# The first layer's feed-forward by Strassen's 2x2 form, with its context rows in two plain passes and one PSUM tile for each product

## The chip, the cores and the metric

The kernel runs on one core of a Trainium2 chip. The metric is the device time of one execution in microseconds (us), as the median of several runs. TensorE (called PE in the profile, with PEld for its weight loads) multiplies a 128x128 weight tile by up to 512 columns at a time into PSUM. VectorE (DVE), ScalarE (ACT) and GpSimd (POOL) do the elementwise work, and SyncE (SP) issues all the transfers of this kernel, in the order of the program.

## The reference, cut to what matters

A trunk of two layers runs over 1024 latent tokens and 256 context tokens, with 1024 features each. Each layer has a mixer and then a gated feed-forward with 2816 hidden features:

```
def swiglu(h, w_in, w_out):
    g, u = jnp.split(h @ w_in, 2, axis=-1)
    return (jax.nn.silu(g) * u) @ w_out

for i in range(DEPTH):                      # DEPTH = 2
    ...                                     # mixer, gated residual
    hl = modulate(rmsnorm(xl, norm_ffn_g[i]), sh2_l, sc2_l)
    xl = xl + g2_l * swiglu(hl, ffn_w_in[i], ffn_w_out[i])
    if not last:
        xc = xc + g1_c * yc
        hc = modulate(rmsnorm(xc, norm_ffn_g[i]), sh2_c, sc2_c)
        xc = xc + g2_c * swiglu(hc, ffn_w_in[i], ffn_w_out[i])
return rmsnorm(xl, norm_final_g)
```

The context goes through the feed-forward in the first layer only, since nothing reads it after the second layer's mixer. All data are fp32. The products must be nearly as exact as fp32, so every operand is split into a high and a low part in the format that TensorE multiplies fast.

## The kernel before, in words

Everything is kept with features on the partitions: `x[d]` is one 128-feature tile of the residual, `h[k]` one of the normed input. Tokens come in three chunks: chunk 0 is the context (256 columns), chunks 1 and 2 are the two halves of the latents (512 columns each). `Row.v(c)` is a tile's part for chunk c.

A weight unit is a 128x1024 tile, eight 128x128 blocks. The class `Stream` (`ws`, lines 205 to 256) hands units out in the one order that is written into `ws.src`: it loads a unit with a transfer into a `raw` buffer (two of these), splits it with `split` (line 258) into `whi` (a copy on ACT, line 259) and `wlo` (a difference on DVE, line 260), and keeps three units split ahead. Every product of a block is three matmuls (lines 329, 330 and 331): high by high, high by low, low by high. So a unit costs 24 matmuls for each chunk that it meets.

The first layer's feed-forward is `ffn` (lines 784 to 830). For each f of the 22 tiles of hidden features it multiplies the gate unit and then the up unit with all three chunks, and after every two f it multiplies the two output units with the hidden tiles and adds each product to `x[d]` on DVE (line 824). Two hidden tiles (f) are thus 6 units, each of which meets three chunks, and 432 matmuls; all 22 are 4752 matmuls, of which 3168 have 512 columns and 1584 have 256.

The second layer's feed-forward works on the latents only and uses Strassen's form with 7 products in place of 8 (lines 1161 to 1364). Weight units are quartered (classes `Block` and `Rows`), quarters are added and subtracted on DVE as they are needed (lines 159 to 165 and 193 to 202), and the input halves are combined once (`h_sums`). For each f there are 7 products of 4 blocks, 84 matmuls of 512 columns (loop at 1262); their results are combined by ACT copies (lines 1273, 1278, 1280, 1282 and 1288) and DVE additions (1275, 1283, 1285, 1286 and 1289). The accumulators are `a`, a PSUM tile of its own, and `b` and `c`, the two halves of one two-bank tile `pb`. Hidden tiles go to DRAM by pairs, again in 7 combinations (`pair_jobs`, `thid`), and the output projection reads them back (`Right`, line 1242) for 77 quarter units of 12 matmuls, 924 matmuls in all (loop at 1327). The first two f of this layer are done plainly, to cover the norm before them.

Small work is interleaved from two lists: `bg` and `slow`. `step(n, m)` runs up to n jobs of the first (a `None` ends the call) and m of the second. `slow` holds the modulation parameters of the next layer (`ada_slow`, lines 408 to 451): 96 loads of 256 KB, 96 groups of DVE multiply-adds (lines 431 and 433), and 24 finishing jobs, each of which transposes on TensorE what DVE has summed (line 438) and reduces it on DVE (439). A norm is a job of statistics on TensorE, ACT and DVE (`Norm.stat`), a broadcast on TensorE (line 498) and eight `norm_apply` jobs (lines 512, 505 and 506). `Norm.feed` squares on ACT and sums on POOL (line 470). Except for SP, whose order is the program's, the order on an engine comes from a planner that goes by the order of the program and by when it believes operands and buffers to be ready.

## Time and profile before

| | us |
|---|---|
| median of 3 runs | 2648.4 |
| the three runs | 2647.07, 2648.4, 2654.0 |
| the profiled execution's own time | 2644.94 |
| its span, first to last instruction | 2643.2 |
| first layer's feed-forward, first to last matmul | 526.37 to 1456.36 |
| second layer's feed-forward, 20 Strassen blocks | about 2018 to 2409 |
| its output projection by Strassen | about 2409 to 2626 |

The span is what the trace covers; the execution's own time is 1.7 us more. Matmuls overlap: each takes about 0.39 us from start to end, but they start much closer together, so the cost of one is the distance between two starts. A busy TensorE in the profile says only that no gap longer than the overlap was seen.

### The profile page before, as it was taken

The numbers are of one execution on the slowest core, as the hardware profiler recorded it, in microseconds if no ns is written. First come the engines' busy times: TensorE is split into PE (matmuls) and PEld (weight loads), VectorE is DVE, ScalarE is ACT, GpSimd is POOL, SyncE is SP. The second block draws the span as 40 slices with busy tenths as digits, with TensorE's granted clock in tenths as the row PEclk, the third lists the DMA queues.
The fourth block names the chain that finished last, engine by engine and source line by source line (L and its number), as shares of the span: only waits on it lengthen the run. The fifth ranks groups of instructions, "written<-read, shape, count | busy, mean of one in ns | idle before, by whom it ended". The sixth has DMA issues, their size and how long they took to land.

```text
span 2643.2 us, 33892 instructions
## 1 busy us (share of the span) xinstructions
PE 2523.7 (95%) x12730; PEld 2103.6 (80%) x12730; DVE 1740.3 (66%) x3182; ACT 1063.3 (40%) x1852; POOL 369.2 (14%) x344
## 2 busy tenths in 40 slices
PE   6999999999999999999999979989999999999997
PEld 3777888788888888888887867778887777777876
DVE  7779857565554554445447658998869556657765
ACT  6685422341111111111115437787745333334453
POOL 2231102200000000000002216555610000000001
PEclk9999999999999999999999999999999999999998
DMA  6112315222122211221112274533252332338352
GB/s 233 56 61 92 104 56 205 74 96 72 44 84 80 80 58 55 88 84 65 67 48 96 97 182 117 128 84 113 91 180 88 104 108 88 105 108 299 98 169 79
DMA packets 134212, 273.39 MB, mean 103 GB/s; under 512 B 13216, under 2 KB 39968, under 8 KB 134048
## 3 DMA queue, kind: packets, MB, share of 16 engines
q1 hardware_dynamic: 134048, 271.22, 31.1%
q8 instruction: 100, 1.64, 0.3%
q14 instruction: 64, 0.52, 0.1%
HBM read 225.82 MB, written 45.35 MB: 103 GB/s over the span
## 4 chain that ended last, share of the span: by engine, by line
PE 77%; DVE 13%; ACT 4%; issue 3%; DMA 3%; POOL 1%; SPq 0%; DVEq 0%; ACTq 0%; POOLq 0%
PE pa L330 14%; PE pa L329 14%; PE pa L331 13%; PE pb L329 10%; PE pb L330 10%; PE pb L331 10%; PE pa L995 2%; DVE s L433 1%; DVE wlo L260 1%; DVE s L964 1%; PE pa L1019 1%; PE pa L1021 1%; DVE s L506 1%; ACT whi L259 1%; PE pb L954 1%
## 5 line engine op out<-in xcount | busy, mean ns | idle before, releaser
L329 PE MATMUL pa<-s,whi 128*128 128x512 f32 (+1 forms) x2086 | 738.0, 355 | 10.9 <-DVE s L724 5.4
L330 PE MATMUL pa<-s,whi 128*128 128x512 f32 (+1 forms) x2086 | 735.1, 353 | 2.7 <-DVE s L260 1.0
L331 PE MATMUL pa<-s,wlo 128*128 128x512 f32 (+1 forms) x2084 | 732.8, 352 | 4.3 <-DVE wlo L260 4.3
L259 ACT ACTIVATE whi<-raw 128x1024 fp32r<-128x1024 f32 (+1 forms) x212 | 199.9, 948 | 660.4 <-issue 267.8
L329 PEld LDWEIGHTS pa<-s,whi 128*128 128x128 f32 x2086 | 398.3, 191 | 65.6 <-DVE s L724 5.6
L331 PEld LDWEIGHTS pa<-s,wlo 128*128 128x128 f32 x2084 | 397.2, 191 | 59.6 <-DVE wlo L260 7.6
L330 PEld LDWEIGHTS pa<-s,whi 128*128 128x128 f32 x2086 | 398.4, 191 | 53.8 <-DVE s L506 1.5
L329 PE MATMUL pb<-s,whi 128*128 128x512 f32 x1022 | 405.0, 398 | 5.3 <-DVE s L623 1.6
L330 PE MATMUL pb<-s,whi 128*128 128x512 f32 x1022 | 400.8, 392 | 4.3 <-DVE s L506 3.6
L331 PE MATMUL pb<-s,wlo 128*128 128x512 f32 x1020 | 399.4, 392 | 0.0
L470 POOL TENSOR_TENSOR s<-s,s 128x512 f32<-128x512 f32 (+1 forms) x87 | 118.9, 1367 | 1838.7 <-ACT s L464 1242.2
L260 DVE TENSOR_TENSOR wlo<-raw,whi 128x1024 fp32r<-128x1024 f32 (+1 forms) x162 | 203.4, 1261 | 125.8 <-ACT whi L259 125.4
L433 DVE SCALAR_TENSOR_TENSOR s<-s,sil,s 128x256 f32<-128x256 f32 x448 | 200.9, 493 | 74.6 <-DMA s<-in_ada_w_dram 72.0
L824 DVE SCALAR_TENSOR_TENSOR s<-pa,mods,s 128x512 f32<-128x512 f32 (+1 forms) x264 | 169.7, 660 | 112.0 <-PE pa L331 111.8
L329 PEld LDWEIGHTS pb<-s,whi 128*128 128x128 f32 x1022 | 192.6, 188 | 54.5 <-ACT s L1282 2.9
L330 PEld LDWEIGHTS pb<-s,whi 128*128 128x128 f32 x1022 | 193.0, 189 | 44.1 <-DVE s L506 6.2
L331 PEld LDWEIGHTS pb<-s,wlo 128*128 128x128 f32 x1020 | 192.5, 189 | 40.8
L329 PE MATMUL pb<-s,wlo 128*128 128x512 f32 x316 | 125.3, 401 | 2.6 <-ACT s L1280 1.3
L989 POOL TENSOR_SCALAR s<-s,small 128x640 f32<-128x640 f32 (+1 forms) x128 | 110.2, 874 | 113.6 <-DVE small L987 60.8
L331 PE MATMUL pb<-s,whi 128*128 128x512 f32 x318 | 124.3, 391 | 0.0
L330 PE MATMUL pb<-s,wlo 128*128 128x512 f32 x316 | 123.1, 390 | 0.0
L976 ACT ACTIVATE s<-s,small 128x640 f32<-128x640 f32 (+1 forms) x128 | 102.2, 799 | 31.2 <-DVE small L964 28.5
(218 smaller groups left out, 3528.3 us busy)
## 6 DMA issues: line engine op xcount, KB each, us to landing
raw<-in_ffn_in_dram SPq DMA_DIRECT2D x100, 512.0 KB, 3.3
s<-in_ada_w_dram SPq DMA_DIRECT2D x144, 256.0 KB, 3.4
thid<-s SPq DMA_DIRECT2D x77, 256.0 KB, 4.5
s<-thid SPq DMA_DIRECT2D x77, 256.0 KB, 2.8
s<-qsp SPq DMA_DIRECT2D x64, 256.0 KB, 4.3
s<-in_ada_w_dram SPq DMA_DIRECT2D x24, 512.0 KB, 9.0
raw<-in_ffn_out_dram SPq DMA_DIRECT2D x24, 512.0 KB, 3.5
qsp<-s SPq DMA_DIRECT2D x96, 128.0 KB, 2.6
```

Of the source, the lines that this page charges most:

```text
L259: ACT.activation(hi, src, AF.Copy)
L260: DVE.tensor_tensor(out=lo, in0=src, in1=hi.bitcast(F32), op=ALU.subtract)
L329: PE.matmul(ps, wh, xh, start=start and i == 0, stop=False, **kw)
L330: PE.matmul(ps, wh, xl, start=False, stop=False, **kw)
L331: PE.matmul(ps, wl, xh, start=False, stop=stop and i == n - 1, **kw)
L433: DVE.scalar_tensor_tensor(out=a, in0=src, scalar=col, in1=a, op0=ALU.mult, op1=ALU.add)
L470: (DVE if q else POOL).tensor_tensor(out=self.acc[q][:, :n], in0=self.acc[q][:, :n], in1=t[:, :n], op=ALU.add)
L506: DVE.scalar_tensor_tensor(out=lo, in0=t, scalar=sh, in1=hi.bitcast(F32), op0=ALU.add, op1=ALU.subtract)
L824: DVE.scalar_tensor_tensor(out=x[d].v(c), in0=ps, scalar=mod(i, 5, d, c), in1=x[d].v(c), op0=ALU.mult, op1=ALU.add)
L976: ACT.activation(p, p, AF.Exp, bias=sm[:, hh : hh + 1], scale=-1.0, accum_out=sm[:, 4 + hh : 5 + hh])
L989: POOL.tensor_scalar(out=self.P[hh + k], in0=self.P[hh + k], scalar1=inv[:, k : k + 1], scalar2=0.0, op0=ALU.mult, op1=ALU.add)
L995: PE.transpose(ps[:, k * P : (k + 1) * P], self.P[k][:, j * P : (j + 1) * P], ident)
```

## The change

The classes and loops of the second layer's Strassen form become a class `Ffn` with methods `sums`, `direct`, `pair_jobs`, `blocks` and `out`, and both layers use it. In the first layer all 22 hidden tiles of the latents go through it (in the second 20, as before). The context rows are done apart: one plain pass over all 44 input units before the blocks, with the hidden tiles stored to DRAM (`chid`), and one plain pass over the 22 output units between the blocks and the Strassen output projection. So the first layer's feed-forward weights are read twice. The residual's latents are stored to DRAM before (`xs`) and read back in `out`. In these plain passes every second unit is loaded into a buffer of the pool `s4` in place of `raw` (`alt`). The next layer's parameter jobs run in the blocks, one to a step in the first eleven, two to a step after. In the blocks of both layers `a`, `b` and `c` are three PSUM tiles of their own. The first norm of the attention layer is put after the sixth product of `out` for chunks 0 and 1, and after `out` for chunk 2.

```diff
@@ Stream
+            self.alt = set()
...
-                    t = wp.tile([P, 1024], F32, tag="raw", name="raw", bufs=2)
+                    if self.nd in self.alt:
+                        t = s4()
+                    else:
+                        t = wp.tile([P, 1024], F32, tag="raw", name="raw", bufs=2)
...
-            self.load_to(i + ahead + (u[0].ahead if isinstance(u, tuple) else 1))
+            self.load_to(i + ahead + (u[0].ahead if isinstance(u, tuple) else 2 if i + ahead + 1 in self.alt or i + ahead in self.alt else 1))
@@ order of the weights
+    FIRST = (0, 2)
...
+    def ffn_plan(i):
+        for _ in range(2):
+            for f in range(FIRST[i]):
+                ws.src += [U_fi[i][f], U_fi[i][NF + f]]
+        for b in B_in[i].values():
+            ws.src += b
+        if i == 0:
+            plain(U_fo[0])
+        ws.src += B_out[i].values()
...
+    plain([U_fi[0][f + q * NF] for f in range(NF) for q in range(2)])
+    ffn_plan(0)
@@ out_group
-                if spill is not None:
-                    SP.dma_start(out=spill[d], in_=x[d].v(c))
+                if c in spill:
+                    SP.dma_start(out=spill[c][d], in_=x[d].v(c))
@@ class Ffn
+        def blocks(self, ns=0):
+            for f, ops in B_in[self.i].items():
+                t, u = s4(), s4()
+                a, b, c = pb()[:, :512], pa(), pa()
...
+                    step(1, ns if f < NF // 2 else 2 * ns)
+                self.hid[f] = [L, R]
+                if f % 2:
+                    bg.extend(self.pair_jobs(f // 2))
...
+        def out(self, x, src, norms, done, mid):
...
+            b = [pa(), pa(), pbs[0][:, :512], pbs[0][:, 512:]]
+            c = [pa(), pa(), pbs[1][:, :512], pbs[1][:, 512:]]
...
+            def full(d, e):
+                norms[e].feed(x[d].v(e))
+                done(d, e)
...
+                if n == "S3":
+                    for d in range(KT):
+                        x[d].lat = s4()
+                        for e in (1, 2):
+                            SP.dma_start(out=x[d].v(e), in_=src[e][d])
...
+                if n == "A22":
+                    mid()
@@ the first layer's feed-forward
+    F = Ffn(0, x)
+    def scaled(d):
+        DVE.scalar_tensor_tensor(out=x[d].v(2), in0=x[d].v(2), scalar=mod(0, 4, d, 2), in1=norms[2].rstd(),
+                                 op0=ALU.mult, op1=ALU.mult)
+    bg.extend([None, norms[2].stat, None, norms[2].bcast])
+    bg.extend([lambda d=d: scaled(d) if d < 4 else norm_apply(norms[2], x, 0, 4, h, d, True) for d in (0, 4, 1, 5, 2, 6, 3, 7)])
+    for k in (0, 1, 3, 2):
+        bg.extend(F.sums(k))
+    for f in range(NF):
+        t = s1()
+        for q in range(2):
+            w, ps = ws.get(U_fi[0][f + q * NF]), pa()[:, :TC]
+            unit_mm(ps, w, h, 0)
+            if q == 0:
+                ACT.activation(t, ps, AF.Silu)
             else:
+                DVE.tensor_tensor(out=t, in0=t, in1=ps, op=ALU.mult)
+                SP.dma_start(out=chid[f], in_=t)
+            step(1)
+    flush(bg)
+    F.direct(h)
+    x, h = [Row(c0=r.c[0]) for r in x], None
+    F.blocks(1)
+    pc = pb(), pb()
+    for t in pc:
+        DVE.memset(t, 0.0)
+    pc = [pc[d // 4][:, d % 4 * TC : d % 4 * TC + TC] for d in range(KT)]
+    cr = Right([chid[f] for f in range(NF)], s1, lambda: (s1(F32R), s1(F32R)), 1, 1)
+    for f in range(NF):
+        w, t = ws.get(U_fo[0][f]), cr.get(f)
+        for d in range(KT):
+            mm(pc[d], [(wcol(w, d), t)], start=False, more=True)
+        step(1, 1)
+    flush(slow)
     norms1 = [Norm(c) for c in range(3)]
+    flush(bg)
+    F.right.ready(0)
+    for d in range(KT):
+        DVE.scalar_tensor_tensor(out=x[d].v(0), in0=pc[d], scalar=mod(0, 5, d, 0), in1=x[d].v(0), op0=ALU.mult, op1=ALU.add)
+        norms1[0].feed(x[d].v(0))
     h1 = new_h()
+    def done0(d, c):
+        SP.dma_start(out=xsp[d][:, (c - 1) * 512 : c * 512], in_=x[d].v(c))
+    F.out(x, xs, norms1, done0, lambda: bg.extend(norm_jobs(norms1[0], x, 1, 1, h1) + norm_jobs(norms1[1], x, 1, 1, h1, True)))
+    flush(bg)
     dump(x, (0, 1, 2), 2)
+    bg.extend(norm_jobs(norms1[2], x, 1, 1, h1, True))
@@ before the last value tiles of the attention layer
+        if c == 2:
+            flush(bg)
         v_tiles(c, wv)
@@ the second layer's blocks, before
-        bc, a = pb(), pa()
-        b, c = bc[:, :512], bc[:, 512:]
```

## Rows read from the trace of the kernel before

**Rows 1.** From the page: busy time of the engines over the span, the TensorE and clock lines of the 40 slices, and the chain of work that ended last.
```profile
PE 2523.7 (95%) x12730; PEld 2103.6 (80%) x12730; DVE 1740.3 (66%) x3182; ACT 1063.3 (40%) x1852; POOL 369.2 (14%) x344
...
PE   6999999999999999999999979989999999999997
...
PEclk9999999999999999999999999999999999999998
...
PE 77%; DVE 13%; ACT 4%; issue 3%; DMA 3%; POOL 1%; SPq 0%; DVEq 0%; ACTq 0%; POOLq 0%
```

**Rows 2.** Sums over stretches: the stretch and its length, busy us and instructions of each engine, granted clock, share of the transfer engines and GB/s. First the whole feed-forward of the first layer, then its steady part, then the slice that holds most of its end.
```profile
526.30:1456.70 930.40, 925.11 (x4846) 794.18 (x4844) 497.74 (x867) 189.35 (x283) 19.06 (x18) 1.00 0.21 73
526.00:1386.00 860.00, 860.00 (x4532) 740.62 (x4531) 448.02 (x784) 148.91 (x217) 1.30 (x1) 1.00 0.21 71
1386.00:1452.00 66.00, 60.71 (x295) 49.95 (x294) 46.28 (x78) 36.74 (x60) 14.27 (x14) 0.97 0.26 93
```

**Rows 3.** Timeline of TensorE: start us, us, engine, line, operation, tiles. First and last of 24 matmuls of 256 columns that open the first layer's feed-forward (the one after them has 512); first and last start of eight of 512 columns in its steady part; its last matmul.
```profile
526.37 0.28 PE L329 MATMUL pa<-s,whi 128*128 128x256 f32 x1
...
529.12 0.28 PE L331 MATMUL pa<-s,wlo 128*128 128x256 f32 x1
...
699.64 0.39 PE L330 MATMUL pa<-s,whi 128*128 128x512 f32 x1
...
701.23 0.39 PE L331 MATMUL pa<-s,wlo 128*128 128x512 f32 x1
...
1456.36 0.39 PE L331 MATMUL pa<-s,wlo 128*128 128x512 f32 x1
```

**Rows 4.** Timeline of the second layer's Strassen blocks: the last evacuation of two successive blocks on ACT, then three waits of TensorE in the last block (in brackets the idle time and what ended it), and the sums over 16 blocks in the columns of rows 2.
```profile
2113.88 0.60 ACT L1288 ACTIVATE s<-pb 128x512 f32<-128x512 f32 x1 [3.16 <-PE pb L331]
...
2133.43 0.60 ACT L1288 ACTIVATE s<-pb 128x512 f32<-128x512 f32 x1 [3.16 <-PE pb L331]
...
2393.72 0.50 PE L329 MATMUL pb<-s,whi 128*128 128x512 f32 x1 [0.69 <-ACT s L1278]
...
2397.98 0.50 PE L329 MATMUL pb<-s,wlo 128*128 128x512 f32 x1 [1.25 <-ACT s L1280]
...
2401.68 0.50 PE L329 MATMUL pb<-s,whi 128*128 128x512 f32 x1 [0.69 <-ACT s L1282]
...
2057.30:2371.90 314.60, 314.60 (x1353) 248.75 (x1352) 188.37 (x291) 120.82 (x210) 0.00 (x0) 1.00 0.31 101
```

**Rows 5.** Groups of DVE instructions by line and shape, from 558 to 1340 us (the steady part of the first layer's feed-forward, which holds all parameter jobs of the second layer): count, busy us, mean ns of one, idle before and what ended it.
```profile
L433 DVE SCALAR_TENSOR_TENSOR s<-s,sil,s 128x256 f32<-128x256 f32 x224 | 100.6, 482 | 73.1 <-DMA s<-in_ada_w_dram 70.5
L260 DVE TENSOR_TENSOR wlo<-raw,whi 128x1024 fp32r<-128x1024 f32 x60 | 72.5, 1220 | 30.0 <-ACT whi L259 29.7
...
L431 DVE TENSOR_SCALAR s<-s,sil 128x256 f32<-128x256 f32 x32 | 10.7, 349 | 16.5 <-DMA s<-in_ada_w_dram 16.4
...
L439 DVE TENSOR_REDUCE small<-pa 128x2 f32<-128x256 f32 x16 | 6.7, 421 | 19.4 <-PE pa L438 19.4
L439 DVE TENSOR_REDUCE small<-pa 128x4 f32<-128x512 f32 x8 | 5.5, 686 | 10.4 <-PE pa L438 10.4
```

**Rows 6.** Sums over four slices of the attention stage, where DVE is busiest, in the columns of rows 2.
```profile
1584.00:1650.00 66.00, 60.52 (x328) 48.68 (x328) 58.96 (x175) 47.01 (x108) 38.30 (x39) 0.95 0.48 126
1650.00:1716.00 66.00, 62.61 (x360) 52.57 (x359) 61.28 (x139) 47.70 (x102) 38.72 (x42) 1.00 0.49 121
1716.00:1782.00 66.00, 59.08 (x342) 48.51 (x342) 65.05 (x164) 56.52 (x132) 36.81 (x41) 0.97 0.32 87
1782.00:1848.00 66.00, 63.85 (x369) 54.08 (x368) 57.58 (x134) 48.62 (x109) 37.98 (x41) 1.00 0.33 108
```

**Rows 7.** Timeline of TensorE at two kinds of seam: a finishing job of the parameters before the feed-forward, and a norm's broadcast at the end of the first layer's feed-forward.
```profile
437.33 0.57 PE L438 MATMUL pa<-ident,s 128*128 128x128 f32 x2 [4.29 <-DVE s L433]
...
1413.31 0.39 PE L498 MATMUL pa<-s,onesr 128*128 128x256 f32 x1 [2.07 <-DVE s L492]
```

**Rows 8.** The second layer's output projection: its sums in the columns of rows 2, and its three longest waits of TensorE before the last product ends.
```profile
2409.00:2626.00 217.00, 210.83 (x928) 172.68 (x926) 154.50 (x239) 102.58 (x180) 13.34 (x9) 1.00 0.46 153
...
2564.95 0.50 PE L330 MATMUL pa<-s,wlo 128*128 128x512 f32 x1 [1.15 <-DVE s L260]
...
2568.95 0.50 PE L330 MATMUL pa<-s,whi 128*128 128x512 f32 x1 [0.99 <-DVE s L260]
...
2598.61 0.61 PE L477 MATMUL pa<-ones,s 128*128 128x1 f32 x4 [2.37 <-POOL s L470]
```

**Rows 9.** Groups by line and shape over the span: the copy of a whole weight unit on ACT, and two steps of a norm's application on DVE for 512 columns.
```profile
L259 ACT ACTIVATE whi<-raw 128x1024 fp32r<-128x1024 f32 x158 | 165.9, 1057 | 621.3 <-issue 267.8 <-PE pb L330 246.2 <-PE pa L330 56.4
...
L506 DVE SCALAR_TENSOR_TENSOR s<-s,mods,s 128x512 fp32r<-128x512 f32 x64 | 51.7, 813 | 1.0 <-ACT s L505 1.0
...
L512 DVE SCALAR_TENSOR_TENSOR s<-s,mods,pa 128x512 f32<-128x512 f32 x64 | 45.2, 740 | 9.1 <-PE pa L498 9.1
```

**Rows 10.** Transfers from 526 to 1456 us: issues by tensor, count, KB each, median us to landing; and the slice with the highest rate, in the columns of rows 2.
```profile
raw<-in_ffn_in_dram SPq DMA_DIRECT2D x48, 512.0 KB, 3.2
s<-in_ada_w_dram SPq DMA_DIRECT2D x96, 256.0 KB, 3.7
...
2376.00:2442.00 66.00, 62.68 (x270) 49.81 (x269) 47.16 (x76) 28.20 (x50) 0.00 (x0) 1.00 0.81 295
```

More of the change, by code (lines that the diff above doesn't have):

```diff
@@ L282, in hybrid_backbone @@
     of = {"xa": xa_, "ga": ga_, "bg": bg_, "cg": cg_, "v": v_, "G": lambda j: U_g[j]}
-    def ffn_seq(chunks):
-        early, late = tuple(c for c in chunks if c != 2), (2,)
-        seq, done_in = [], 0
-        for o in range(0, NF, 2):
-            upto = min(o + 3, NF)
-            new = list(range(done_in, upto))
-            done_in = upto
-            if o == 0:
-                seq += [("in", f, early) for f in new[:2]] + [("in", f, late) for f in new[:2]]
-                new = new[2:]
-            seq += [("in", f, early if f >= NF - 2 else chunks) for f in new]
-            if o < NF - 2:
-                seq.append(("out", (o, o + 1), chunks))
-        t = (NF - 2, NF - 1)
-        return seq + [("out", t, early)] + [("in", f, late) for f in t] + [("out", t, late)]
@@ L732, in hybrid_backbone, with out_group @@
     dump(Y, (0, 1, 2), 0)
-    def out_group(h, x, units_, chunks, i, m, norms, nb=3, ns=0, spill=None):
+    def out_group(h, x, units_, chunks, i, m, norms, spill, nb=3, ns=0):
         for d in range(KT):
@@ L773, in hybrid_backbone @@
     ada_slow([(0, 5, 2)], True)
[L774 removed]
+    xs = {c: dp.tile([KT, P, 512], F32, name="xs") for c in (1, 2)}
+    out_group(yh, x, U_ro, (0, 1), 0, 2, norms, xs, 3, 2)
     h = new_h()
[L776 to L777 removed]
+    bg.extend(norm_jobs(norms[0], x, 0, 4, h) + norm_jobs(norms[1], x, 0, 4, h, True))
+    out_group(yh, x, U_ro, (2,), 0, 2, norms, xs)
     flush(bg)
@@ L832, in hybrid_backbone @@
-    xsp = dp.tile([KT, P, TL], F32, name="xsp")
-    ada_slow([(1, m, 2 if m < 2 else 1) for m in (1, 0, 2, 3, 4, 5)], False)
-    norms1 = [Norm(c) for c in range(3)]
-    h1 = new_h()
-    def done0(c, d):
-        norms1[c].feed(x[d].v(c))
-        if c:
-            SP.dma_start(out=xsp[d][:, (c - 1) * 512 : c * 512], in_=x[d].v(c))
-        step(2)
-        if d == KT - 1:
-            bg.extend(norm_jobs(norms1[c], x, 1, 1, h1, wait=3 if c == 0 else 1, gap=2 if c == 0 else 1))
-    bg.extend(norm_jobs(norms[2], x, 0, 4, h))
@@ L846, in hybrid_backbone, with __init__, load_to, get @@
-    ffn(0, h, x, ffn_seqs[0], done0, {})
-    flush(slow)
+    OP = dict(A11="B11", A12="B21", S2="T2", S3="T3", S1="T1", A22="T4", S4="B22")
+    KEYS = list(OP.values())
+    class Right:
+        def __init__(self, src, raw, pair, ahead, look):
+            self.src, self.raw, self.pair, self.ahead, self.look = src, raw, pair, ahead, look
+            self.nl = self.ns = 0
+            self.t, self.w = {}, {}
+        def load_to(self, i):
+            while self.nl <= min(i, len(self.src) - 1):
+                t = self.t[self.nl] = self.raw()
+                SP.dma_start(out=t, in_=self.src[self.nl])
+                self.nl += 1
+        def get(self, i):
+            self.ready(i)
+            return self.w.pop(i)
+        def ready(self, i):
+            while self.ns <= min(i + self.ahead, len(self.src) - 1):
+                self.load_to(self.ns + self.look)
+                w = self.w[self.ns] = self.pair()
+                split(*w, self.t.pop(self.ns))
+                self.ns += 1
@@ new lines, in hybrid_backbone @@
+    ada_slow([(1, m, 2 if m < 2 else 1) for m in (1, 0, 2, 3, 4, 5)], False)
+    xsp = dp.tile([KT, P, TL], F32, name="xsp")
+    chid = dp.tile([NF, P, TC], F32, name="chid")
+    F = Ffn(0, x)
[4 more added lines that the diff above has]
+    bg.extend([lambda d=d: scaled(d) if d < 4 else norm_apply(norms[2], x, 0, 4, h, d, True) for d in (0, 4, 1, 5, 2, 6, 3, 7)])
@@ L1298, in hybrid_backbone @@
+    bg.extend([sums[k][3] for k in range(4)] + F.pair_jobs(0))
+    F.blocks()
     norms2 = [Norm(c, two=2 if c > 1 else 1) for c in range(3)]
```

361 lines of the change are left out of this document (139 added, 222 removed).

## The prediction, made before the change was built or run

> **What bounds the kernel now.** I read the page first [rows 1]: TensorE is busy for 95% of the span, its slices are at nine tenths or more from the eighth on but for two seams, the granted clock stands at its upper level, and 77% of the chain that ended last is TensorE. So a matmul less is time less, wherever TensorE does not wait. Next came the sums by stage [rows 2]: in the first layer's feed-forward TensorE is never idle from 526 to 1386 us, with DVE at 448 of 860 and the transfers at a fifth of what they can do; all that this stage wastes lies at its end, 930.4 - 925.1 = 5.3 us idle and a clock of 0.97 over 66 us, 2 us more. So this stage is bound by its count of matmuls and by nothing else. The timeline gives their price [rows 3]: 1.59 us for seven of 512 columns, 0.227 us each, and 2.75 us for 23 of 256, 0.1196 each. As a check, 3168 x 0.227 + 1584 x 0.1196 = 719.1 + 189.4 = 908.5 us, in a stage of 1456.6 - 526.4 = 930.2; the rest is the waste above, 64 transposes of parameters and three norms, which stay.
>
> **Matmuls removed.** Latents before: 22 x 2 x 8 x 2 x 3 = 2112 for the input and 1056 for the output. After: 22 x 84 = 1848 and 77 x 12 = 924. That is 396 fewer of 512 columns, 396 x 0.227 = **-89.9 us**. The context's 1584 of 256 columns are only moved. The Trainium skill ("TensorE: Matmul & The Clock Gate", section on the back-to-back issue gap) gives columns over 2.4 GHz plus 2.5 ns, an estimated 216 ns for 512 columns; by that the term would be 85.5 us. The rows say 227 ns, and I go by them.
>
> **Waste of the old stage.** Its 5.3 us of waits and 2 us of slow clock [rows 2], of which one wait is the 2.07 us before a norm's broadcast [rows 7], go with the old end of the stage: **-7**. What comes instead is counted by place below.
>
> **Context input pass, added by itself.** 44 units of 24 matmuls, 2.87 us each, 126 us. Before, a unit served all three chunks, 2.87 + 2 x 5.45 = 13.8 us; now ACT and DVE must split one every 2.87 us. ACT's copy is 1.06 us [rows 9] and DVE's difference 1.22 [rows 5]. Beside them run 28 jobs, one to a unit: norm of chunk 2 and input sums. A norm job is 0.74 + 0.81 us on DVE [rows 9]; with the difference and half a gate product (at most 0.24, half of a 256-column operation of 0.48, rows 5) it makes 3.0 us against 2.87, some 4 us late over 28 units, of which part is covered by the two units split ahead. A 512 KB load lands in 3.2 us and a unit each 2.87 us is 183 GB/s; the transfers have reached 295 [rows 10], and with the extra buffers three or four units are in flight. **+3**, bounds 0 and 12.
>
> **The 22 blocks.** 22 x 84 x 0.227 = 419.5 us of TensorE. DVE is the question. In the second layer's blocks it is busy 188.4 of 314.6 us, 0.599 [rows 4], so 251 us here. Into the same blocks go all parameter jobs, which before were spread over 780 us: 100.6 + 10.7 + 12.2 = 123.5 us [rows 5]. Together 375 of 419.5, 89%; and since in the second half of the blocks they run two to a step and end in ten blocks, there 11.4 + 6.2 = 17.6 of 19.07 us, 92%. The nearest rows of a DVE that busy are in the attention [rows 6]: at 0.87 to 0.93 TensorE was idle for 3 to 8%, which here is 13 to 35 us. There every matmul waits for fresh results of DVE; in the blocks the weights are split six quarters, 16 us, ahead, so I take less. What is behind a late DVE: the finishing transposes stand in TensorE's own queue, and one such wait was 4.29 us [rows 7]. What is behind SP: a store of a hidden pair waits for DVE's difference, behind it the next parameter load, which lands in 3.7 us [rows 10], and behind that DVE's next job one step (2.72 us) later. **+10**, bounds 0 and 35.
>
> **Seams.** Start of the blocks; blocks to context output pass, where the accumulators are zeroed on DVE after the last Silu has read theirs; and that pass to `out`. The waits of such a kind are 0.69 to 2.07 us [rows 4, 7]. The context output pass itself is 63 us with 1.22 us of DVE and 1.06 of ACT for each 2.87, without other jobs to speak of, so at TensorE's pace. Three seams at 2 us, **+6**, bounds 0 and 16.
>
> **The output projection.** 924 x 0.227 = 209.7; in the second layer it takes 217.0, so 7.3 are lost, among them 1.15 + 0.99 behind the burst of additions after the fifth product and 2.37 for POOL's norm sums [rows 8]. The last is due to the final norm and is not asked for so early here. In its place the seventh product carries eight norm applications of chunk 0 and five of chunk 1, about 14 us of DVE where the second layer has 8 x 0.74 = 6. DVE is at 154.5 of 217, 71%, so of 30 us it has 9 free and gets 8 more plus the statistics: about 4 us late. 7.3 - 2.4 + 4 = **+9**, bounds 5 and 18.
>
> **PSUM tiles in the second layer.** A block takes 2133.43 - 2113.88 = 19.55 us and its matmuls 84 x 0.227 = 19.07. The 0.48 us are waits too short to show as idle; in the last block ACT is later and they show: the product that starts in one half of the two-bank tile waits 0.69, 1.25 and 0.69 us for ACT to read the other half [rows 4]. With tiles apart nothing is shared. 20 x 0.48 + 2.6 = **-12**, bounds -12 and 0. Against this the Trainium skill ("PSUM — Partial Sum Buffer", section on bank collisions) lets engines clash only within one bank; the halves are two banks, so by it no wait was needed and the term is 0. The rows show the wait all the same, so it is the tile that is guarded, not the bank; the rule is a rival below.
>
> **Residual stored and read back.** 16 stores and 16 loads of 256 KB on SP, both beside matmuls: the stores sit before the next weight loads and wait for DVE; **+1**, bounds 0 and 5.
>
> **Sum.** -89.9 - 7 + 3 + 10 + 6 + 9 - 12 + 1 = -79.9 on the profiled execution's own 2644.9, so 2565. The median of the runs is 3.5 above that execution, which gives **2568**. With every term at its good end it would be 2545, with every term at its bad end 2637.
>
> **Rivals.** (a) *DVE becomes the bound in the blocks.* For: 92% in the second half, and the parameter jobs of before also waited 70.5 us for their loads [rows 5]; if these waits stay, DVE has 375 + 70 = 445 us in blocks of 419.5. Against: a DVE that is late finds its load landed. Then the blocks cost +25 to +35 in place of +10: 2583 to 2593. (b) *The PSUM tiles bring nothing*, because the bank is what counts or because another wait is next: 12 us less, 2580. For: no single wait shows in a steady block; against: the three that show in the last. (c) *Slower: the context passes starve.* One mechanism: 66 weight units that must be loaded and split each for 24 short matmuls. If a unit is not ready every 2.87 us, all of that is on the path. The gain of 80 is eaten at 80 / 66 = 1.21 us more, at 4.1 us a unit; with a single buffer in turn a unit would take 3.2 + 1.06 + 1.22 = 5.5 us, so it takes two buffers out of step to stay under. At 4.5 us the time is 2568 + 66 x 1.63 - 3 = 2673. For: the load lands in 3.2 us, more than 2.87. Against: at least three units in flight, and 183 GB/s asked of 295 seen.
>
> **Chances.** Forecast 0.62, its own range 2550 to 2581. (a) 0.18, (b) 0.12, (c) 0.05; 0.03 for better than 2550. The range 2550 to 2600 holds the forecast, (b) and most of (a), and leaves out (c), the best cases and the far end of (a). A measurement of this kernel tells 0.3%, 8 us, from no change: faster 0.93, same 0.02, slower 0.05.
>
> **What would show it.** Right: the blocks of the second layer at 19.1 us each; the first layer's from 19.1 to 20 with DVE near 0.9; context units at 2.9 us; no wait of TensorE over 5 us between the passes; the stage in about 860 us. Wrong: blocks of the first layer at 20.2 or more and TensorE waiting at line 438 (rival a); second-layer blocks still at 19.55 (b); units at over 4 us with DVE waiting for the load (c).

## The result, and the profile after

Median 2577.05 us (2574.02 to 2580.39) against 2649.2 us (2647.07 to 2654.0) for the kernel before: ratio 0.9725, 95% interval 0.9707 to 0.9744. That is 72 us less, where 80 were forecast. The profiled execution after took 2580.39 us (span 2578.5), 3.3 above its median, and the one before 2644.94, 4.3 below, so the two traces differ by only 64.6 us. The sums below are made between the traces. In the kernel after, the three matmuls of a product stand in lines 323 to 325, the split in 263 and 264, the quarter sums in 160 and 267, and the parameter jobs in 425, 427 (multiply-adds) and 432 (transposes).

The page of the kernel after, the lines that answer to [rows 1]: busy time, the TensorE and clock lines of the slices, and the lines of DVE and the transfers.

```profile
PE 2440.5 (95%) x12334; PEld 2045.2 (79%) x12334; DVE 1913.3 (74%) x3481; ACT 1257.9 (49%) x2214; POOL 373.1 (14%) x344
...
PE   6999999999999999999998989989999999999997
...
DVE  7788856686778888759567668998868666667665
...
PEclk9999999999999999999999989999999999999998
DMA  6112325346344455578243274522432333239142
```

There are 12730 - 12334 = 396 matmuls fewer, as worked out, and DVE has gone from 66 to 74% of a shorter span. TensorE is still at nine tenths almost everywhere, so the slices tell little; the stages do. Sums over stretches of the kernel after in the columns of [rows 2], cut at its first matmul of each stage: context's input pass, 22 blocks, context's output pass, output projection, the first projections of the second layer, that layer's 20 blocks, its output projection.

```profile
526.60:662.50 135.90, 131.85 (x1068) 131.14 (x1067) 102.52 (x139) 74.83 (x105) 1.30 (x1) 0.97 0.55 186
662.50:1107.50 445.00, 434.43 (x1915) 353.76 (x1914) 355.76 (x705) 161.19 (x286) 0.00 (x0) 0.99 0.48 159
1107.50:1170.80 63.30, 63.30 (x529) 63.30 (x528) 39.16 (x53) 31.60 (x47) 0.00 (x0) 1.00 0.82 277
1170.80:1390.60 219.80, 214.77 (x943) 176.30 (x942) 163.01 (x258) 111.41 (x200) 24.68 (x17) 0.99 0.46 159
1390.60:1416.10 25.50, 21.29 (x107) 18.09 (x106) 20.07 (x36) 13.91 (x25) 7.28 (x5) 0.87 0.37 125
1950.40:2337.20 386.80, 382.35 (x1682) 314.83 (x1680) 248.47 (x381) 158.00 (x274) 0.00 (x0) 1.00 0.35 117
2337.20:2559.80 222.60, 216.62 (x934) 177.78 (x934) 154.09 (x239) 102.36 (x179) 12.35 (x9) 0.98 0.43 150
```

The last three stretches in the kernel before, whose 20 blocks begin at 2008.1 us (for its first layer see [rows 2]):

```profile
1456.70:1474.90 18.20, 18.18 (x108) 15.99 (x107) 12.13 (x22) 9.98 (x19) 8.62 (x6) 1.00 0.57 203
2008.10:2407.30 399.20, 392.54 (x1682) 309.16 (x1681) 245.71 (x382) 157.31 (x273) 0.00 (x0) 1.00 0.34 112
2407.30:2624.40 217.10, 212.16 (x935) 174.10 (x933) 153.54 (x239) 101.22 (x178) 12.35 (x8) 1.00 0.47 155
```

The first layer's feed-forward went from 930.4 to 864.0 us (the first four stretches), the second layer's blocks from 399.2 to 386.8. Two places that no step of the forecast had got longer: the projections behind the stage, 18.2 to 25.5, and the second layer's output projection, 217.1 to 222.6. Together -66.4 - 12.4 + 7.3 + 5.5 = -66.0 of the span's -64.7.

Where TensorE stood, from its timeline in the kernel after: three waits in the input pass, with two of the matmuls behind the second, the first matmul of the last of the 22 blocks and the wait in it for the end of the parameter jobs, the third chunk's norm behind the stage, the start of the second layer's output projection.

```profile
534.65 0.39 PE L323 MATMUL pa<-s,whi 128*128 128x256 f32 x1 [1.02 <-ACT small L473]
...
536.27 0.44 PE L325 MATMUL pa<-s,wlo 128*128 128x256 f32 x1 [1.12 <-DVE wlo L264]
536.50 0.42 PE L323 MATMUL pa<-s,whi 128*128 128x256 f32 x1
536.72 0.42 PE L324 MATMUL pa<-s,whi 128*128 128x256 f32 x1
...
545.21 0.50 PE L492 MATMUL pa<-s,onesr 128*128 128x512 f32 x1 [1.91 <-DVE s L486]
...
1081.49 0.39 PE L323 MATMUL pb<-s,whi 128*128 128x512 f32 x1
...
1086.94 0.69 PE L432 MATMUL pa<-ident,s 128*128 128x128 f32 x2 [3.71 <-DVE s L427]
...
1401.51 1.65 PE L471 MATMUL pa<-ones,s 128*128 128x1 f32 x7 [3.73 <-POOL s L464]
...
2337.16 0.72 PE L323 MATMUL pa<-s,wlo 128*128 128x512 f32 x2 [1.72 <-ACT s L263]
```

Behind 536.27 the matmuls of 256 columns start 0.22 us apart instead of 0.12. The same places by their granted clock; the line from 1081.50 is the whole last block:

```profile
536.00:539.00 3.00, 2.73 (x13) 2.73 (x14) 3.00 (x6) 1.38 (x3) 0.00 (x0) 0.58 0.00 0
...
1081.50:1107.50 26.00, 22.29 (x88) 17.97 (x87) 15.21 (x26) 8.65 (x14) 0.00 (x0) 0.87 0.56 193
1086.00:1094.00 8.00, 7.05 (x20) 5.70 (x21) 3.55 (x8) 1.12 (x2) 0.00 (x0) 0.57 0.54 169
1400.00:1407.00 7.00, 5.49 (x22) 5.08 (x23) 3.37 (x8) 1.86 (x4) 1.46 (x1) 0.51 0.52 191
2337.00:2343.00 6.00, 5.84 (x18) 4.39 (x19) 2.72 (x5) 2.32 (x6) 0.00 (x0) 0.72 1.05 402
```

Around these waits the clock was at its lower level (1.2 GHz) for some us. Such matmuls count as busy, so the price of a wait is more than its idle time: behind the stage 25.5 - 18.2 = 7.3 us, of which 3.7 is the wait. The last block took 26.0 us, and the 21 before it 419.0, 19.95 each; so the mean of 445.0 / 22 = 20.2 is pulled up by the last one.

### The profile page after: what moved, and what is told of

Its sections match the earlier page's. It is cut to its first block, busy times and chain, and to the rows that moved or that the text cites. A ratio compares the mean times of both kernels' runs of the same rounds, so it can differ in the third digit from the quotient of the medians.

```text
span 2578.5 us, 34620 instructions
## 1 busy us (share of the span) xinstructions
PE 2440.5 (95%) x12334; PEld 2045.2 (79%) x12334; DVE 1913.3 (74%) x3481; ACT 1257.9 (49%) x2214; POOL 373.1 (14%) x344
## 5 line engine op out<-in xcount | busy, mean ns | idle before, releaser
L323 PE MATMUL pa<-s,whi 128*128 128x512 f32 (+1 forms) x1746 | 626.3, 360 | 12.1 <-DVE s L718 5.4
L325 PE MATMUL pa<-s,wlo 128*128 128x512 f32 (+1 forms) x1746 | 623.6, 358 | 5.0 <-DVE wlo L264 5.0
L324 PE MATMUL pa<-s,whi 128*128 128x512 f32 (+1 forms) x1746 | 622.5, 357 | 5.6 <-DVE s L264 4.6
L323 PEld LDWEIGHTS pa<-s,whi 128*128 128x128 f32 x1746 | 336.4, 193 | 60.5 <-DVE s L718 5.6
L325 PEld LDWEIGHTS pa<-s,wlo 128*128 128x128 f32 x1746 | 336.2, 193 | 53.5 <-DVE wlo L264 8.6
L324 PEld LDWEIGHTS pa<-s,whi 128*128 128x128 f32 x1746 | 335.9, 192 | 50.1 <-DVE s L264 5.5
L324 PE MATMUL pb<-s,whi 128*128 128x512 f32 (+1 forms) x766 | 283.3, 370 | 3.6 <-DVE s L500 3.6
L323 PE MATMUL pb<-s,whi 128*128 128x512 f32 (+1 forms) x766 | 283.7, 371 | 1.9 <-DVE s L617 1.6
L325 PE MATMUL pb<-s,wlo 128*128 128x512 f32 (+1 forms) x766 | 281.9, 368 | 0.0
L323 PE MATMUL pa<-s,wlo 128*128 128x512 f32 x658 | 260.1, 396 | 11.5 <-ACT s L886 5.4
L324 PE MATMUL pa<-s,wlo 128*128 128x512 f32 x658 | 258.0, 392 | 0.9 <-DVE s L264 0.9
L325 PE MATMUL pa<-s,whi 128*128 128x512 f32 x658 | 257.0, 391 | 0.0
L263 ACT ACTIVATE whi<-s 128x512 fp32r<-128x512 f32 (+1 forms) x152 | 109.7, 722 | 154.6 <-PE pb L325 92.3
L324 PEld LDWEIGHTS pb<-s,whi 128*128 128x128 f32 x766 | 146.2, 191 | 27.8 <-DVE s L500 6.2
L323 PEld LDWEIGHTS pb<-s,whi 128*128 128x128 f32 x766 | 145.8, 190 | 25.9 <-issue 1.7
L323 PEld LDWEIGHTS pa<-s,wlo 128*128 128x128 f32 x658 | 124.4, 189 | 43.0 <-ACT s L886 9.0
L324 PEld LDWEIGHTS pa<-s,wlo 128*128 128x128 f32 x658 | 124.6, 189 | 27.2 <-DVE s L264 1.9
```

What stands on the lines that cost most here:

```text
L263: ACT.activation(hi, src, AF.Copy)
L323: PE.matmul(ps, wh, xh, start=start and i == 0, stop=False, **kw)
L324: PE.matmul(ps, wh, xl, start=False, stop=False, **kw)
L325: PE.matmul(ps, wl, xh, start=False, stop=stop and i == n - 1, **kw)
```

## The experiments

All totals are medians of four runs; the kernel before, run beside each group, was at 2650.6 to 2652.0 (at 2649.2 beside the kernel after). "Blocks" is the stretch from the first layer's first block to its context output pass in the profiled run.

| kernel | total us | ratio to before | blocks us |
|---|---|---|---|
| after | 2577.1 | 0.9725 (0.9707 to 0.9744) | 445.0 |
| shared_psum | 2600.3 | 0.9806 (0.9792 to 0.9821) | 457.0 |
| psum_only | 2636.0 | 0.9943 (0.9928 to 0.9957) | none |
| right_s2 | 2573.4 | 0.9709 (0.9694 to 0.9723) | 445.4 |
| no_ada | 2552.4 | 0.9629 (0.9613 to 0.9645) | 418.9 |
| half_math | 2556.5 | 0.9646 (0.9630 to 0.9662) | 431.2 |
| ada_ahead | 2570.6 | 0.9700 (0.9682 to 0.9718) | 436.8 |
| spread | 2568.5 | 0.9689 (0.9670 to 0.9707) | 426.7 |
| pool_queue | 2596.8 | 0.9798 (0.9781 to 0.9815) | 461.5 |
| no_alt | 2599.9 | 0.9806 (0.9785 to 0.9827) | 439.1 |
| norm_gaps | 2565.8 | 0.9684 (0.9666 to 0.9702) | 443.1 |
| best_sp | 2551.0 | 0.9625 (0.9609 to 0.9640) | 428.3 |
| best_pool | 2567.4 | 0.9686 (0.9670 to 0.9700) | 445.9 |

**The PSUM tiles, undone and done alone (shared_psum, psum_only).**

```diff
 shared_psum, in the kernel after
-                a, b, c = pb()[:, :512], pa(), pa()
+                bc, a = pb(), pa()
+                b, c = bc[:, :512], bc[:, 512:]
 psum_only, in the kernel before
-        bc, a = pb(), pa()
-        b, c = bc[:, :512], bc[:, 512:]
+        a, b, c = pb()[:, :512], pa(), pa()
```

> The changed kernel, but the blocks of both layers take their second and third PSUM areas out of one two-bank tile again, as the kernel before did in its second layer. Theory (a product that starts in one half of a shared tile waits for the copy out of the other half): the period of the second layer's 20 blocks goes from 19.04 back to about 19.55 us, 10 to 13 us in all; the first layer's 22 blocks, with a period of 20.2, lose between 0 (the wait lies inside one that is there already) and 11 us. Total 2587 to 2601. Rival (the shorter period comes from elsewhere, from the order of tiles or transfers): period stays 19.04, total 2574 to 2580.

> The kernel before with one edit alone: three PSUM tiles in its second-layer blocks, one for each area, instead of one tile of two banks and one of a bank. Theory: blocks 10 to 13 us shorter, total 2636 to 2639 against 2649. For the 8.6 us that the changed kernel lost behind its last block: if that loss follows from the shorter blocks (an earlier start of the output projection), the time from the last block's Silu to the end rises here as well, from 234.4 to about 243, and the total gains only 2 to 5 us; if it comes from the new pair tiles or the new order of banks in the output projection, it stays at 234 to 236. Rival on the tiles: 0, total 2647 to 2651.

The last evacuation of two successive blocks of the second layer on ACT, in the kernel after, in shared_psum and in psum_only:

```profile
2105.17 0.60 ACT L892 ACTIVATE s<-pa 128x512 f32<-128x512 f32 x1 [2.03 <-PE pa L325]
2124.21 0.60 ACT L892 ACTIVATE s<-pa 128x512 f32<-128x512 f32 x1 [2.03 <-PE pa L325]
```
```profile
2106.78 0.60 ACT L893 ACTIVATE s<-pb 128x512 f32<-128x512 f32 x1 [3.17 <-PE pb L325]
2126.36 0.60 ACT L893 ACTIVATE s<-pb 128x512 f32<-128x512 f32 x1 [3.17 <-PE pb L325]
```
```profile
2088.71 0.60 ACT L1287 ACTIVATE s<-pa 128x512 f32<-128x512 f32 x1 [2.03 <-PE pa L331]
...
2107.75 0.60 ACT L1287 ACTIVATE s<-pa 128x512 f32<-128x512 f32 x1 [2.03 <-PE pa L331]
```

19.04 us with three tiles in either kernel, 19.58 with the shared one, against 84 x 0.2267 = 19.04 for the matmuls alone. Both totals, 2600.3 and 2636.0, are where the theory has them. So the whole 0.5 us per block was the shared tile, which the steady block of the kernel before did not show as a wait anywhere [rows 4]. In the first layer it comes to about as much: 457.0 - 445.0 = 12.0 us, where kernels that leave these blocks as they are (after, right_s2, norm_gaps, no_alt) lie between 439.1 and 445.4. The Trainium skill ("PSUM — Partial Sum Buffer", section "PSUM bank collisions raise a hardware error") has engines clash within one bank only; b and c are two banks, so it asks for no wait, and these rows show that the program waits for the tile all the same.

By TensorE's first matmul of each stage, psum_only shortens the second layer's blocks from 399.2 to 386.2 and lengthens the output projection behind them from 217.1 to 220.4. So this edit alone brings 3.3 us there, of the 5.5 that the changed kernel lost. Counted from the last block's Silu, as in the expectation, it is 239.8 against 234.4, between the two answers named.

```profile
2010.40:2396.60 386.20, 382.14 (x1682) 314.83 (x1680) 248.56 (x381) 158.25 (x274) 0.00 (x0) 1.00 0.34 117
2396.60:2617.00 220.40, 215.72 (x934) 176.58 (x934) 154.15 (x239) 101.07 (x178) 12.34 (x8) 0.98 0.46 152
```

TensorE's busy time in the projection rose from 212.16 to 215.72 us with the clock down from 1.00 to 0.98: most of what came back is clock. The clock varies in this stage: kernels with the same projection as the kernel after took 220.7 us (shared_psum, with the old tile in its blocks) to 222.7 (no_alt). Why the clock falls there and did not in the kernel before is open.

**The right-hand pairs (right_s2).**

```diff
-            self.right = Right([...], s2, pair4, 2, 3)
+            self.right = Right([...], s2, pair4 if i == 0 else lambda: (s2(F32R), s2(F32R)), 2, 3)
```

> The changed kernel, but the right-hand pairs of the second layer's output projection are two tiles of 512 columns each again, as before, instead of one tile that holds both. Theory (the extra 8.6 us behind the last block come from the pair tiles, which share a pool of 17 with the weight rows and the residual): the time from the last block's Silu to the end falls from 243 to 234 to 237, total 2568 to 2573. Rival (they come from the new order of the PSUM banks, or from where the short dips of the granted clock happen to fall): 241 to 245, total 2574 to 2580.

The projection takes 220.3 us instead of 222.6, as in psum_only; from the last Silu to the end it is 240.8, neither answer. That the pair tiles account for the 2.3 us is not shown: the difference is no larger than what this stage varies by, and best_sp, which has the same edit, takes 222.1. The total, 2573.4, cannot be told from the kernel after: the intervals overlap.

**The parameter jobs (no_ada, half_math).** no_ada leaves out the second layer's parameter jobs. half_math leaves out half of the multiply-adds of both layers: line 427 has 128 of them instead of 224 before 519 us, too, since the first layer's slabs go through the same code.

```diff
 no_ada
-    ada_slow([(1, m, 2 if m < 2 else 1) for m in (1, 0, 2, 3, 4, 5)], False)
+    DVE.memset(mods[:, 1, :, :, :], 0.5)
 half_math
-            for kk in range(nk):
+            for kk in range(nk if wide else 1):
```

> The changed kernel without the second layer's modulation parameters: they are set to a constant, and the 217 background jobs that compute them (loads, multiply-adds on VectorE, transposes) are left out, most of which ran in the first layer's 22 blocks. Theory (these jobs in VectorE's queue make the first layer's blocks 20.2 us long): the period falls to 19.0 to 19.3, the blocks from 445 to 419 to 427 us (7 us of the fall are the jobs' own transposes and the wait at the end of them), total 2551 to 2561. Rival (the blocks are long because of the first layer's own work: the stores of pair sums, weight splits, context): period stays at 19.9 or more, total 2568 to 2574.

> The changed kernel with every second multiply-add of the second layer's parameters left out (one of the two blocks of 256 columns in each slab), so that VectorE has about 55 us less to do in the first layer's blocks, while all slabs are loaded and read in the same order and all transposes stay. Theory 1 (what counts is how full VectorE's queue is: splits and quarter sums come late when it is 0.8 busy): its busy share in the blocks falls from 0.80 to about 0.68 and TensorE's loss in them from 18.5 to under 6 us, blocks 425 to 432, total 2558 to 2567. Theory 2 (what counts is that VectorE stands until a slab lands): the idle time on slabs stays at 30 us or more, and the blocks stay at 438 to 446, total 2570 to 2579.

The first layer's blocks in no_ada, then in half_math:

```profile
662.10:1081.00 418.90, 418.90 (x1850) 346.84 (x1850) 258.30 (x392) 166.88 (x286) 0.00 (x0) 1.00 0.33 109
```
```profile
654.10:1085.30 431.20, 429.40 (x1914) 352.21 (x1913) 307.78 (x577) 162.89 (x286) 0.00 (x0) 1.00 0.50 164
```

Without the jobs the blocks take 1848 x 0.2267 = 418.9 us and TensorE never stands. All that they cost above that, 445.0 - 418.9 = 26.1 us, is due to the parameter jobs: 65 instructions more on TensorE (1915 against 1850), nearly all transposes of about 0.11 us, so 7 us, and 19 us of waiting. Of the 19, 7 lie in the last block, 3.7 of wait for the last transposes and the lower clock behind them; the other 12 are spread over 21 blocks. half_math keeps every load, every slab's place in the queue and every transpose, and drops half of the multiply-adds. DVE's share falls from 355.8 / 445.0 = 0.80 to 307.8 / 431.2 = 0.71, and the waiting from 19 to 431.2 - 418.9 - 7 = 5 us. The idle time of DVE that ends on a slab did not fall; it rose. Waits of DVE from 663 to 1087 us, line and what it waited for (us in total, times, longest), kernel after and half_math:

```profile
DVE s L427 <- DMA s<-in_ada_w_dram: 24.0, 18, 2.1
DVE whi L264 <- ACT whi L263: 22.6, 20, 1.9
DVE wlo L264 <- ACT wlo L263: 10.3, 16, 1.1
```
```profile
DVE s L427 <- DMA s<-in_ada_w_dram: 31.5, 20, 3.7
DVE wlo L264 <- ACT wlo L263: 22.5, 24, 2.4
DVE whi L264 <- ACT whi L263: 21.2, 21, 2.2
```

So theory 1 holds here, and theory 2 as it was worded does not: with less work DVE waits as long for slabs, and TensorE hardly at all. Half of the gain is the end of the parameter jobs (last block 19.2 instead of 26.0), half the other 21 blocks (412.1 instead of 419.0; 417.3 to 423.0 in the kernels that leave them as they are). The stage began at 519.2 instead of 526.6; the halved multiply-adds of the first layer stand ahead of it, and what else is in these 7 us was not taken apart.

How it reaches TensorE, in one block of the kernel after: the timelines of DVE, ACT and TensorE, and under them TensorE's waits in all these blocks.

```profile
814.76 1.28 DVE L427 SCALAR_TENSOR_TENSOR s<-s,sil,s 128x256 f32<-128x256 f32 x3 [1.93 <-DMA s<-in_ada_w_dram]
...
817.55 0.69 DVE L267 TENSOR_TENSOR raw<-s,raw 128x512 f32<-128x512 f32 x1
```
```profile
818.27 0.63 ACT L263 ACTIVATE whi<-raw 128x512 fp32r<-128x512 f32 x1 [4.58 <-DVE raw L267]
818.81 0.58 ACT L886 ACTIVATE s<-pa 128x512 f32<-128x512 f32 x1
```
```profile
819.44 0.50 PE L323 MATMUL pa<-s,wlo 128*128 128x512 f32 x1 [1.01 <-ACT s L886]
```
```profile
PE pa L323 <- ACT s L886: 6.3, 10, 1.0
PE pa L432 <- DVE s L427: 4.3, 2, 3.7
```

DVE does parameter work between its quarter sums (lines 160 and 267); ACT stands 4.58 us for the sum that it has to split; the copy of the fifth product (line 886) is behind this split in ACT's queue; and the seventh product, which goes into the same accumulator, waits for the copy. Here a slab's landing began it, 1.93 us. These visible waits are 6.3 of the 12 us in the 21 blocks; that the rest goes the same way is not shown. In half_math such landings cost DVE more, 31.5 us, but TensorE's waits for the copy fall to 1.6.

**Loads further ahead, jobs dealt out otherwise, another queue (ada_ahead, spread, pool_queue).**

```diff
 ada_ahead
-        out = [lambda: load(0)]
+        out = [lambda: load(0)] + ([] if wide else [lambda: load(1)])
+        far = 1 if wide else 2
...
-            if q + 1 < len(todo):
-                out.append(lambda q=q: load(q + 1))
+            if q + far < len(todo):
+                out.append(lambda q=q: load(q + far))
 spread
-            step(1)
+            step(1, 2 if f >= NF // 2 else 0)
...
-                    step(1, ns if f < NF // 2 else 2 * ns)
+                    step(1, ns)
 pool_queue
-            SP.dma_start(out=tiles[q], in_=ada_w[...])
+            (SP if wide else POOL).dma_start(out=tiles[q], in_=ada_w[...])
```

> The changed kernel with the parameter slabs loaded two ahead instead of one. Theory 1 (what lengthens the first layer's blocks is that VectorE stands in its queue until a slab lands: 25 us of its idle time in the 22 blocks ends on these loads): that idle time falls under 6 us, the period from 20.2 to 19.3 to 19.7, total 2561 to 2570. Theory 2 (it is the number of VectorE instructions between ScalarE's splits and the quarter sums, and not the landing): the idle time on loads goes too, but the period stays at 19.9 to 20.3, total 2573 to 2579.

> The changed kernel with the 217 parameter jobs dealt out otherwise: two after each step of the second half of the context's input pass (44 in all), one after each step of all 22 blocks (before: one in the first 11, two in the others), the rest in the context's output pass. Theory 1 (VectorE's landing waits, worst where load and use stand in one step): the last 11 periods fall from 20.2 to 19.3 to 19.7, blocks 8 to 12 us shorter; the input pass, whose VectorE is 0.6 busy there, gains 0 to 3 us of loss; total 2566 to 2572. Theory 2 (the load on VectorE as such): late blocks 3 to 6 us shorter, first blocks about the same, total 2571 to 2576. Rival (the jobs cost the same wherever they stand): 2575 to 2580.

> The changed kernel with the loads of the second layer's parameter slabs issued by POOL, which has nothing else to do in the first layer's blocks, instead of SP. Theory (SP takes its queue in order; each block's weight load stands there up to 14 us until VectorE has read the last quarter out of the two raw buffers, and the slab loads behind it go out late and in one burst with the weights): VectorE's idle time that ends on slabs falls from 33 us in the 22 blocks to under 8, the blocks from 445 to 428 to 437 us, total 2561 to 2570. Rival 1 (the slabs land late because of the rate, not of the queue): idle time on slabs stays over 20 us, total 2574 to 2580. Rival 2 (POOL's own issuing of a load costs more, or VectorE and POOL get into each other's way): blocks longer, total above 2582.

ada_ahead is inconclusive by its own terms: DVE's idle time on slabs (lines 425 and 427) fell from 33.5 to 25.3 us, not under 6, and the blocks gained 8.2. Most of the 8.2 is the last block, 19.2 us instead of 26.0; the 21 before it take 417.6, as in the kernels that leave them as they are. spread brought the blocks to 426.7 us, 18.3 less, which is more than either of its theories said (21 blocks 407.4, the last one 19.3), with 22.7 us of that idle time left. It gave back 2.6 us in the input pass and 0.7 in the output pass; the 2.2 in the output projection are no more than what other kernels differ by there. The share of DVE in its blocks is 324.5 / 426.7 = 0.76: less work for DVE, less waiting, as in half_math, but with somewhat shorter waits for slabs too, so spread alone does not tell the theories apart.

pool_queue moves the first layer's 48 slabs as well, 144 loads in all. It refutes the theory on SP's queue. The slabs landed in 3.5 us after their issue instead of 5.7, but DVE's idle time on them stayed at 28 us. Waits in its blocks, DVE and POOL:

```profile
DVE s L427 <- DMA s<-in_ada_w_dram: 23.1, 18, 4.1
DVE s L267 <- DMA thid<-s: 22.4, 12, 4.3
...
POOL s L411 <- DVE s L427: 259.3, 69, 17.3
```

POOL itself stood before a load until DVE had done with an earlier slab (69 times), so the loads follow DVE and not the queue. The blocks became 16.5 us longer, as rival 2 has it, though not for its reasons as far as the trace shows them: a load costs POOL 0.55 us, and DVE's multiply-adds take 481 ns against 484. TensorE waited 20.0 us for the copy of line 886, with the clock at 0.98 over the 461.5 us. The share of DVE in these blocks is 349.9 / 461.5 = 0.76, the same as in spread, so the share alone does not decide. DVE's wait for the stores of the hidden sums grew from 5.8 to 22.4 us. Why taking loads off SP makes these stores later was not settled.

**The context's passes with two buffers (no_alt).**

```diff
-        ws.alt.update(range(n + 1, len(ws.src), 2))
```

> The changed kernel with the weights of the context's two passes in two raw buffers alone, as elsewhere, instead of every second one in a tile of the large pool. It tells what the rival case of starving passes would cost. If a buffer's turn (landing 3.2 to 4 us, split about 1.4) has to fit into two units of 2.87 us: 5.0 to 6 us against 5.74, so 2.87 to 3.1 us per unit, 0 to 10 us in the 66 units, total 2577 to 2587. If the landing in these passes grows with the rate of 200 to 300 GB/s beyond 5 us: 3.3 us or more per unit, 28 us or more, total above 2605.

Between the two answers: input pass 145.6 instead of 135.9 us, output pass 76.8 instead of 63.3, so 23 us, or 0.22 and 0.61 us a unit. The loads still land in 3.5 to 3.6 us, so a buffer's turn holds more than landing and split; what else was not taken apart, nor why the blocks between the passes came out 5.9 us shorter, 4.2 of them in the last block (21.8 us). The edit also takes away the second load ahead, which `get` asks for only where a unit is in `alt`; buffers and order together are worth 23 us, and passes without them would not have eaten the gain of 80.

**The third chunk's norm later (norm_gaps).**

```diff
-    bg.extend([None, norms[2].stat, None, norms[2].bcast])
+    bg.extend([None] * 2 + [norms[2].stat] + [None] * 3 + [norms[2].bcast])
...
-    bg.extend(norm_jobs(norms1[2], x, 1, 1, h1, True))
+    bg.extend(norm_jobs(norms1[2], x, 1, 1, h1, True, wait=3))
```

> The changed kernel with the statistics of the third chunk put later in both places where TensorE waits for them: two steps before and three behind them at the start of the context's input pass (one and one now), and three steps before them after the first layer's output projection (one now). Theory (TensorE, which takes its instructions in order, stands there until the norm's sums are ready, and the granted clock halves for a few us behind such a stand): the start of the pass loses 2 to 4 us instead of 8, the projections behind the stage 0 to 2 us instead of 7; total 2566 to 2571. Rival (the norm is what the following work needs anyway, so the wait only moves): 2575 to 2579.

The input pass and the projections behind the stage:

```profile
526.70:660.10 133.40, 131.41 (x1067) 130.70 (x1066) 102.83 (x139) 74.77 (x105) 1.30 (x1) 0.97 0.55 189
1386.70:1405.60 18.90, 18.07 (x106) 15.63 (x104) 17.53 (x26) 11.37 (x18) 7.35 (x5) 1.00 0.47 168
```

The projections went from 25.5 to 18.9 us, back to what they took before, with the clock at 1.00 again. The input pass gained only 2.5 (in kernels that leave it as it is it takes 134.4 to 135.9): the wait for the broadcast is gone, another of 1.7 us for the first norm's application came in front, and the clock still fell.

**Together (best_sp, best_pool).** best_sp has the edits of norm_gaps, spread, ada_ahead and right_s2, and splits the second layer's first right-hand pair inside its last block; best_pool has POOL's queue in place of ada_ahead.

```diff
                     if f == NF - 1 and key == "S2":
                         self.right.load_to(2)
+                    if self.i and f == NF - 1 and key == "A22":
+                        self.right.ready(-2)
```

> The changed kernel with five edits together: later statistics at both places, slabs two ahead, parameter jobs dealt out otherwise, the second layer's right-hand pairs in two tiles, and the first of these pairs split inside the last block. If the gains add (start 2.5 and projections 6.6 and 3 behind them, blocks 18, less 4 given back in the context's two passes, right pairs 2, first split 2): 30 us, total 2547 to 2555. If they overlap (each moves the same waits on): 2556 to 2566.

> The same five edits, but instead of slabs two ahead they are issued by POOL, one ahead. If the place in SP's queue is what makes slabs late, this has the blocks at 424 to 427 us and the total is 2544 to 2553; if POOL's issuing is dear, 2556 or more.

best_sp is at 2551.0 us, 26 us under the kernel after and in the range named for gains that add. In the first layer's blocks they do not: 428.3 us, where spread alone has 426.7. The fifth edit took away the wait of 1.7 us ahead of the second layer's output projection, but the projection then took 222.1 us where right_s2 took 220.3, so no gain in sum is shown. Its first layer's blocks:

```profile
661.60:1089.90 428.30, 425.84 (x1893) 350.30 (x1892) 326.33 (x605) 164.45 (x288) 0.00 (x0) 1.00 0.45 149
```

428.3 - 418.9 - 43 x 0.11 = 5 us of waiting are left of 19. best_pool confirms that POOL's queue is the wrong place: 17.6 us more in the blocks.

## Why the prediction was right, step by step

- **Matmuls removed: right.** 396 fewer, and no_ada's blocks show the price without anything beside them: 418.9 / 1848 = 0.2267 us. By the formula of the Trainium skill that the prediction weighed ("TensorE: Matmul & The Clock Gate", section "Back-to-back issue gap"), an estimated 216 ns each, they would have taken 399 us; the trace does not agree.
- **Context input pass: right in kind, small in size.** 135.9 us less 126.3 of matmuls and some 1.5 for the norm's own leaves 8, forecast 3 (bounds 0 and 12). Not a late DVE over 28 units, as worked out, but three waits for norm and weights in the first 20 us and the clock behind them; from 550 us on TensorE never stood.
- **Waste of the old stage: too small.** -7 was taken. By the prices above, the 930.4 us hold 907.6 of matmuls; less 7 for transposes and 4 for norms, some 12 are left that the old stage lost.
- **The 22 blocks: right in kind, mis-sized.** +19 where +10 was taken (bounds 0 and 35). The mechanism is the one of rival (a): the parameter jobs in DVE's queue, shown by no_ada and half_math. Its signs were there in part: the mean period of 20.2 us is 19.95 in 21 blocks, inside what the forecast named for itself, and 26.0 in the last, where TensorE waited for the transposes. The working had DVE at 375 us of work and a share of 0.89; it was 355.8 and 0.80, and already there TensorE lost 4%. The rival's own price, 25 to 35, rested on waits for slabs that add to DVE's work in full; half_math shows that they do not. The 0.5 us of the shared tile would have come on top (shared_psum).
- **Seams: wrong, and cheap.** +6 forecast (bounds 0 and 16), nothing measured: the context's output pass is busy for all its 63.3 us and 528 x 0.1196 = 63.1.
- **Output projection: right.** 219.8 less 924 x 0.2267 and 2.5 for norms is 8, forecast 9.
- **PSUM tiles: right.** -12.4 in the second layer (bounds -12 and 0). The forecast took them as a net gain, and 3.3 us came back in the output projection behind. The rival in which they bring nothing is out.
- **Residual stored and read back: not seen apart.** +1 was taken (bounds 0 and 5). DVE waited 4.7 us in the first layer's projection for the loads, and TensorE shows no wait on them.
- **Not in the sum.** The projections behind the stage, +7.3: the third chunk's last four tiles are now complete only after the seventh product, all at once, where the old stage finished that chunk tile by tile; POOL sums their squares, and TensorE stands in its queue for the statistics. And 5.5 us in the second layer's output projection, mostly a lower clock, whose cause is open. The forecast priced what lies inside the changed stages and not what is handed on behind them.
- **The sum.** Inside the first layer's stage the errors nearly cancel: -66.4 measured, -67.9 forecast, with 5 too little for the input pass and 9 for the blocks against 6 too much for the seams and 5 too little gained from the old waste. That is in part luck. With the tiles it is -78.8, and what went missing of the 79.9 is the 12.8 us behind the two stages. So the profiled execution took 2580 us where 2565 was forecast. The medians, 2577 against 2568, look better, because each profiled execution lies some us off its own median, in opposite directions.
- **Rival (c)** is out: the output pass runs at 2.88 us a unit with 277 GB/s; no_alt says that without the extra buffers and the second load ahead the two passes would have cost 23 us more.

## What to carry to other kernels

What this program waits for is a tile: two accumulators in one PSUM tile cost TensorE 0.5 us per block of 84 matmuls even in separate banks, and no wait in the steady state shows it; only the period against the matmul count does. When background work moves into a shorter stage, look at the engine that prepares operands: the jobs cost 26 us in these blocks, and with half of their multiply-adds 12, though VectorE waited as long for its loads. Its busy share alone does not tell the price: at 0.76 TensorE lost some 3 us in spread and some 35 in pool_queue. Look at the end of such work as well: 7 of the 19 us of waiting lay in the one block in which the jobs ended. And follow the last result of a stage into the next one: a norm's statistics two steps too early in TensorE's queue cost 7 us.

## What the runs showed that was not expected

- A wait of TensorE of 1 to 4 us often cost about twice its length, because the granted clock was at its lower level behind it (0.51 to 0.72 in the stretches above). In other places the same wait cost only itself: [rows 8] has 1.15 and 0.99 us in a stretch with the clock at 1.00.
- The first layer's feed-forward began at 525.9 to 529.4 us in the profiled runs of kernels with no edit ahead of it, and its blocks took 439.1 to 445.4 where they were not edited, most of the difference in the last one. The totals of the kernel before alone go from 2646.2 to 2656.3. A gain of a few us has to be read from its stretch, and against what that stretch varies by.
- Taking the parameter slabs' loads off a queue that stands most of the time made the kernel 20 us slower, not faster.
